# Dealing stretches of rows to SBUF partitions in another order in a row-wise maximum kernel

## The chip, the cores and the metric

The kernel runs on one core of one Trainium2 chip. The metric is the device time of one execution in microseconds (us), the median of several runs. One further execution was taken by the hardware profiler; the profile page and all views of the trace are of that one.

## The reference

The input `x` has 8192 rows of 8192 float32, 268.4 MB in all. The result is one number for each row, the largest absolute value in it:

```python
def reference(x: np.ndarray) -> np.ndarray:
    return np.linalg.norm(x, ord=np.inf, axis=1)
```

## The kernel before

**Layout.** Every row is reduced inside one SBUF partition. The rows are cut into two groups, `GROUPS = [46, 18]`. The first group is the first 46 x 128 rows of `x`, the second the remaining 18 x 128. Inside a group each partition has one stretch of neighbouring rows: 46 rows (1.5 MB, contiguous in `x`) in the first group, 18 rows (0.59 MB) in the second. Partition p has stretch p. This is made in lines 48 and 49: `x_of[f]` is a view of `x` with one row for each partition, its stretch, and `out_of[f]` is the same view of the result.

**Loads.** `load(pos, w)` (line 97) brings in the next `w` columns of every partition's stretch. It picks a place in `ring`, a tile with room for three loads of 16384 columns (64 KiB in each partition), and issues one transfer on SP's queue at line 108. The last load goes to a tile of its own, `last`. There are 39 loads. `WHOLE` lists the large ones: two of 8192 columns, thirty of 16384 (two rows of each partition, 8.39 MB), one of 8192. `LAST` lists the short ones that make up each partition's last row: 3920, 1984, 1040, 576, 320 and 352 columns. Since the loads use the ring in turn, a load may only be issued when the reduce of the load three places before it has ended; this wait stands on SP's queue ahead of the transfer. The calls to `declare_no_dep` at line 115 drop waits on earlier loads that those reduces already order.

**Reduces.** VectorE (DVE) does nearly all of the work: `absmax`, recorded at line 68, one instruction for each whole load, 128 partitions by one or two rows, into `res`, which has one column for each row of a partition. Near the end `shared` splits a row: VectorE takes its first part, while ScalarE (ACT, line 90) takes absolute values of the other parts and GpSimd (POOL, line 75) takes their maximum. Everything is emitted in a fixed order (`keep`).

**Stores.** When the last row is reduced (line 153), SP stores its 128 results at line 154. The other columns of `res` are stored a little earlier by two transfers from ScalarE's queue at line 159, one for each group. A store writes one run of numbers for each partition: 46 numbers in the first group, 17 in the second, and one in the last store.

Of the kernel before, what the change touches and what calls it, by code (L numbers as in the profile page):

```python
# [1 line left out]

# [4 lines left out]

P = 128
FP32 = mybir.dt.float32
INT32 = mybir.dt.int32  # L10
MAX = mybir.AluOpType.max
X = mybir.AxisListType.X
ABS = mybir.ActivationFunctionType.Abs

GROUPS = [46, 18]


WHOLE = (
    [(8192, ())] * 2 + [(16384, ())] * 29 + [(16384, (3712, 3680)), (8192, (2016, 1984))]
)
LAST = [
    (3920, (1680,)), (1984, (848,)), (1040, (432,)), (576, (240,)), (320, ()), (352, ())
]
RING = 3 * 16384


@with_exitstack  # L30
def kernel(
    ctx: ExitStack,
    tc: tile.TileContext,
    x: bass.AP,
    out: bass.AP,
):
    nc = tc.nc
    n_rows, n_cols = x.shape
    R = n_rows // P
    assert R == sum(GROUPS) and n_cols == 8192  # L40
    keep = tc.keep_in_program_order


    first = []
    x_of, out_of = {}, {}
    for k in GROUPS:
        f = len(first)
        x_of[f] = x[f * P : (f + k) * P].rearrange("(p r) m -> p (r m)", r=k)
        out_of[f] = out[f * P : (f + k) * P].rearrange("(p r) -> p r", r=k)
        first += [f] * k  # L50

    single = ctx.enter_context(tc.tile_pool(name="single", bufs=1))

    ring = single.tile([P, RING], FP32)
    res = single.tile([P, R], FP32)

    n_parts = sum(1 + len(g) for w, g in LAST[:-1])
    last = single.tile([P, LAST[-1][0] + n_parts], FP32)

    def not_before(inst, other, why):  # L60
        tc.add_manual_dep(
            inst.ins, other.ins.name,
            mybir.DependencyInfo(mybir.DependencyClass.Sync, mybir.DependencyReason.DATA),
            reason=why,
        )

    def absmax(dst, src):
        return keep(nc.vector.tensor_reduce(  # L68
            out=dst, in_=src, axis=X, op=MAX, apply_absolute_value=True,
        ))  # L70

    def max_pool(dst, src):

        pool = nc.gpsimd
        keep(pool.add_instruction(  # L75
            mybir.InstTensorReduce(
                name=nc.get_next_instruction_name(),
                ins=[pool.lower_ap(src.bitcast(INT32))],
                outs=[pool.lower_ap(dst.bitcast(INT32))],
                op=MAX,  # L80
                axis=X,
            )
        ))

    def shared(part, buf, g):

        a = buf.shape[1] - sum(g)
        red = absmax(part[:, :1], buf[:, :a])
        for i, c in enumerate(g):
            keep(nc.scalar.activation(buf[:, a : a + c], buf[:, a : a + c], ABS))  # L90
            max_pool(part[:, 1 + i : 2 + i], buf[:, a : a + c])
            a += c
        return red

    loads = []

    def load(pos, w):

        row = pos // n_cols
        a = pos - first[row] * n_cols  # L100
        if pos + w == R * n_cols:
            buf = last[:, :w]
        else:
            at = loads[-1][0] + loads[-1][1] if loads else 0
            if at + w > RING:
                at = 0
            buf = ring[:, at : at + w]
        inst = nc.sync.dma_start(out=buf, in_=x_of[first[row]][:, a : a + w]).ins  # L108
        if pos + w < R * n_cols:
            if (len(loads) + 4) % 10 < 5:  # L110


                for b, v, earlier in loads:
                    if b < at + w and at < b + v:
                        tc.declare_no_dep(
                            inst, earlier, reason="ordered by the reduces in between",
                        )
            loads.append((at, w, inst))
        return buf


    pos = 0
    for u, (w, g) in enumerate(WHOLE):
        buf = load(pos, w)
        row, k = pos // n_cols, w // n_cols
        pos += w
        whole = k - 1 if g else k
        if whole:
            red = absmax(
                res[:, row : row + whole],  # L130
                buf[:, : whole * n_cols].rearrange("p (c m) -> p c m", m=n_cols),
            )
        if g:
            part = single.tile([P, 1 + len(g)], FP32, name=f"part{u}")
            shared(part, buf[:, whole * n_cols :], g)
            max_pool(res[:, row + whole : row + k], part)
        if u == 1:

            not_before(
                keep(nc.scalar.activation(res[:, :1], res[:, :1], ABS)),  # L140
                red, "not before the second row is in",
            )


    n = LAST[-1][0]
    for h, (w, g) in enumerate(LAST[:-1]):
        buf = load(pos, w)
        pos += w
        shared(last[:, n : n + 1 + len(g)], buf, g)
        n += 1 + len(g)  # L150

    load(pos, LAST[-1][0])
    absmax(res[:, R - 1 :], last)
    final = nc.sync.dma_start(out=out_of[first[-1]][:, GROUPS[-1] - 1 :], in_=res[:, R - 1 :])


    for f, o in out_of.items():
        k = min(o.shape[1], R - 1 - f)
        early = keep(nc.scalar.dma_start(out=o[:, :k], in_=res[:, f : f + k]))
        tc.add_manual_dep(  # L160
            early.ins, final.ins.name,
            mybir.DependencyInfo(
                mybir.DependencyClass.NoSync, mybir.DependencyReason.SCHED_ONLY
            ),
            reason="takes the later semaphore",
        )


# [1 line left out]
_INS = ['x']  # L170
_OUTS = [((8192,), 'float32')]


# [23 lines left out]
```

## Time and profile before

| | |
|---|---|
| median of 3 runs | 627.39 us (627.34 to 627.58) |
| the profiled execution, whole | 627.43 us |
| its span, first to last instruction | 625.7 us |
| VectorE busy in the span | 536.7 us, 86% |
| ScalarE, GpSimd busy | 15.1 us, 14.1 us |
| bytes read from HBM | 268.44 MB |
| instructions | 175 |

The span is the part of an execution that the trace covers; the remaining 1.7 us lie around it. "Busy" is time in which an engine executes; a transfer's time "to landing" runs from its issue to the last of its bytes, and includes the time that it stands behind earlier transfers.

### The profile page before, as it was taken

The numbers are of one execution on the slowest core, as the hardware profiler recorded it, in microseconds if no ns is written. First come the engines' busy times: TensorE is split into PE (matmuls) and PEld (weight loads), VectorE is DVE, ScalarE is ACT, GpSimd is POOL, SyncE is SP. The second block draws the span as 40 slices with busy tenths as digits, with TensorE's granted clock in tenths as the row PEclk, the third lists the DMA queues.
The fourth block names the chain that finished last, engine by engine and source line by source line (L and its number), as shares of the span: only waits on it lengthen the run. The fifth ranks groups of instructions, "written<-read, shape, count | busy, mean of one in ns | idle before, by whom it ended". The sixth has DMA issues, their size and how long they took to land.

```text
span 625.7 us, 175 instructions
## 1 busy us (share of the span) xinstructions
DVE 536.7 (86%) x40; ACT 15.1 (2%) x10; POOL 14.1 (2%) x14
## 2 busy tenths in 40 slices
DVE  1938988889888899888898888988889888899888
ACT  0000000000000000000000000000000000000044
POOL 0000000000000000000000000000000000000026
DMA  8999999999999999999999999999999999999997
GB/s 369 436 469 402 469 402 469 402 469 402 469 402 457 415 415 457 402 469 402 469 402 469 402 469 402 469 402 453 419 415 457 402 469 402 469 402 469 402 436 304
DMA packets 6048, 268.47 MB, mean 429 GB/s; under 512 B 1056, under 2 KB 1312, under 8 KB 1696
## 3 DMA queue, kind: packets, MB, share of 16 engines
q1 hardware_dynamic: 5760, 268.44, 99.3%
q10 hardware_dynamic: 288, 0.03, 0.0%
HBM read 268.44 MB, written 0.03 MB: 429 GB/s over the span
## 4 chain that ended last, share of the span: by engine, by line
DMA 71%; DVE 28%; SPq 0%; issue 0%; DVEq 0%
DMA ring<-in_x_dram 71%; DVE res L68 28%; DVE last L68 1%; SPq L108 0%; DVEq L68 0%
## 5 line engine op out<-in xcount | busy, mean ns | idle before, releaser
L68 DVE TENSOR_REDUCE res<-ring 128x2 f32<-128x16384 f32 (+1 forms) x32 | 525.4, 16420 | 86.4 <-DMA ring<-in_x_dram 86.4
L90 ACT ACTIVATE ring<-ring 128x3712 f32<-128x3712 f32 (+7 forms) x8 | 13.6, 1719 | 577.2 <-DMA ring<-in_x_dram 573.9
L75 POOL TENSOR_REDUCE part<-ring 128x1 int32<-128x3712 int32 (+3 forms) x4 | 10.1, 2562 | 607.6 <-ACT ring L90 607.6
L68 DVE TENSOR_REDUCE part<-ring 128x1 f32<-128x800 f32 (+1 forms) x2 | 5.5, 2748 | 0.1
L68 DVE TENSOR_REDUCE last<-ring 128x1 f32<-128x2240 f32 (+4 forms) x5 | 5.3, 1115 | 0.1
L75 POOL TENSOR_REDUCE last<-ring 128x1 int32<-128x1680 int32 (+3 forms) x4 | 3.4, 855 | 0.6 <-ACT ring L90 0.4
L140 ACT ACT_TABLE_LOAD x1 | 1.3, 1283 | 0.7 <-PEq L181 0.7
L140 ACT ACTIVATE res<-res 128x1 f32<-128x1 f32 x1 | 0.2, 203 | 29.3 <-DVE res L68 29.3
L68 DVE TENSOR_REDUCE res<-last 128x1 f32<-128x361 f32 x1 | 0.5, 529 | 0.1
L75 POOL TENSOR_REDUCE res<-part 128x1 int32<-128x3 int32 x2 | 0.4, 198 | 0.1
L181 POOL MEMSET const-float32-0.0<- 128x1 f32 x1 | 0.1, 99 | 0.2 <-issue 0.2
L181 POOL MEMSET const-bfloat16-1.0<- 128x1 bf16 x1 | 0.1, 102 | 0.0
L181 POOL MEMSET const-uint8-127<- 128x1 uint8 x1 | 0.1, 101 | 0.0
L181 POOL MEMSET const-float32-1.0<- 128x1 f32 x1 | 0.1, 99 | 0.0
## 6 DMA issues: line engine op xcount, KB each, us to landing
ring<-in_x_dram SPq DMA_DIRECT2D x3, 4096.0 KB, 21.4
ring<-in_x_dram SPq DMA_DIRECT2D x1, 1960.0 KB, 35.4
ring<-in_x_dram SPq DMA_DIRECT2D x1, 992.0 KB, 37.4
ring<-in_x_dram SPq DMA_DIRECT2D x1, 520.0 KB, 38.2
ring<-in_x_dram SPq DMA_DIRECT2D x30, 40.8
ring<-in_x_dram SPq DMA_DIRECT2D x1, 288.0 KB, 38.4
last<-in_x_dram SPq DMA_DIRECT2D x1, 176.0 KB, 38.3
ring<-in_x_dram SPq DMA_DIRECT2D x1, 160.0 KB, 38.3
```

Of the source, the lines that this page charges most:

```text
L68: return keep(nc.vector.tensor_reduce(out=dst, in_=src, axis=X, op=MAX, apply_absolute_value=True,))
L75: keep(pool.add_instruction(mybir.InstTensorReduce(name=nc.get_next_instruction_name(), ins=[pool.lower_ap(src.bitcast(INT32))], outs=[poo ...
L90: keep(nc.scalar.activation(buf[:, a : a + c], buf[:, a : a + c], ABS))
L140: keep(nc.scalar.activation(res[:, :1], res[:, :1], ABS)),
L181: nc = _bacc.Bacc("TRN2", target_bir_lowering=False, num_devices=1)
```

## The change

In both groups the stretches are numbered q x 16 + g, with q from 0 to 7 and g from 0 to 15, and the view puts g ahead of q. The partition with number 8g + q thus has stretch 16q + g, instead of stretch 8g + q. The views have one axis more: `x_of[f]` has the axes (g, q, columns), `out_of[f]` has (g, q, rows). Each load reads the same bytes as before in the same number of pieces, and each row's result is stored in its place; the tiles, the reduces and the order of all instructions stay as they are.

```diff
     for k in GROUPS:
         f = len(first)
-        x_of[f] = x[f * P : (f + k) * P].rearrange("(p r) m -> p (r m)", r=k)
-        out_of[f] = out[f * P : (f + k) * P].rearrange("(p r) -> p r", r=k)
+        x_of[f] = x[f * P : (f + k) * P].rearrange("(q g r) m -> g q (r m)", g=16, r=k)
+        out_of[f] = out[f * P : (f + k) * P].rearrange("(q g r) -> g q r", g=16, r=k)
         first += [f] * k
...
-        inst = nc.sync.dma_start(out=buf, in_=x_of[first[row]][:, a : a + w]).ins
+        inst = nc.sync.dma_start(out=buf, in_=x_of[first[row]][:, :, a : a + w]).ins
...
-    final = nc.sync.dma_start(out=out_of[first[-1]][:, GROUPS[-1] - 1 :], in_=res[:, R - 1 :])
+    final = nc.sync.dma_start(out=out_of[first[-1]][:, :, GROUPS[-1] - 1 :], in_=res[:, R - 1 :])
...
     for f, o in out_of.items():
-        k = min(o.shape[1], R - 1 - f)
-        early = keep(nc.scalar.dma_start(out=o[:, :k], in_=res[:, f : f + k]))
+        k = min(o.shape[2], R - 1 - f)
+        early = keep(nc.scalar.dma_start(out=o[:, :, :k], in_=res[:, f : f + k]))
```

In the built program a load's destination was an access of 128 partitions by w elements and is now 128 by 1 by w; its source was 128 stretches by w and is now 16 by 8 stretches by w. A store's destination becomes 16 by 8 by its row count.

## The prediction, made before the changed kernel had run

> **What bounds the kernel now.** I read the page's busy table first (VectorE 86%, so no compute engine is full), then its DMA queues, then the chain of waits, then the waits of SP's queue, and last the stretch from 100 to 560 us alone.
>
> ```profile
> DVE 536.7 (86%) x40; ACT 15.1 (2%) x10; POOL 14.1 (2%) x14
> ...
> q1 hardware_dynamic: 5760, 268.44, 99.3%
> q10 hardware_dynamic: 288, 0.03, 0.0%
> ```
>
> The queue of loads has 99.3% of the time of all 16 DMA engines: 0.993 x 625.7 = 621.3 us, and 4.4 us of the span lie outside it. One engine moves 64 KiB in 621.3 / (268.44 MB / 16 / 65536 B) = 621.3 / 256 = 2.43 us, or 27.0 GB/s.
>
> ```profile
> DMA ring<-in_x_dram 71%; DVE res L68 28%; DVE last L68 1%; SPq L108 0%; DVEq L68 0%
> ...
> 59.17 40.78 DMA ring<-in_x_dram
> 99.95 0.02 issue
> 99.97 17.23 DVE res L68
> 117.20 0.02 issue
> 117.22 40.79 DMA ring<-in_x_dram
> 158.01 0.02 issue
> 158.03 17.23 DVE res L68
> ```
>
> The chain gives VectorE 28%, which misleads. A transfer takes 40.8 us from issue to landing, but 58.03 us go by for three loads, so loads land every 19.34 us and each waits about 21 us behind an earlier one. VectorE's 17.2 us lie on the chain only because they free the ring's place.
>
> ```profile
> SPq L108 <- DVE res L68: 517.7, 29, 19.0
> ...
> DVE res L68 <- DMA ring<-in_x_dram: 51.1, 24, 2.1
> ...
> 100.00:562.30 462.30, 413.24 (x24) 0.00 (x0) 0.00 (x0) 1.00 1.00 433
> ```
>
> (The first two lines are total us, times and longest of a wait, on SP's queue and in the steady part; the third is a stretch, its length, the busy time of DVE, ACT and POOL, the clock, the DMA share and GB/s.) In the steady part VectorE waits 2.1 us for each load and never the other way round; the engines' share is 1.00 at 433 GB/s. Thus the rate of the 16 DMA engines sets the time, and whatever lengthens a transfer shows at full size, since only 2.1 us of each period are VectorE's to give.
>
> [...]
>
> **The change, part by part.**
>
> Nothing is removed or moved: the same 39 loads and 3 stores, in the same places of the same queues, with the same bytes, no new wait. VectorE, ScalarE and GpSimd run as before.
>
> Issue of a transfer. SP's first load occupies its queue for 0.38 us, later ones 0.33 to 0.53. A two-axis source may take longer to set up; no row shows it. From below nothing, from above a doubling, 0.4. Loads in mid-stream have a load and more queued ahead (40.8 us to landing against 19.34 a load), so only the first load and the final store lie on the path: 0 to 0.8 us, and I take 0.4. The two stores on ScalarE's queue lie beside the last reduces; doubling them from 0.86 us together exposes at most the same again.
>
> Read order. Neighbours in g read places 46 x 32 KiB = 1.44 MiB apart (0.56 MiB in the second group). [...] to the start I allow 0.8 us more, since the first load lands 12.1 us after issue against 4.19 MB / 433 GB/s = 9.7 of payload. From the other side, clashes could cost[...]. I take 0.
>
> Write order, the part that decides. [...] The trace's packet records have the first packets of the 16 engines starting over 0.58 us[...]. I take 2.5%, near the small end[...].
>
> Sum on the profiled execution: stream 2 x 621.3 = 1242.6; less 2.5% of 621.3 = 15.5; plus the 4.4 us outside the stream and 0.4 for issue: span 1231.9. With 627.43 - 625.7 = 1.7 around it, 1233.6; I say 1233. The profiled execution is 0.04 us above the median shown, so nothing is corrected. VectorE's 17.2 us then fit into a period of about 38 us; what is late is always the load, also at the end, where the short loads land at half pace and VectorE no longer trails them.
>
> Range of this case: f from 6% (1212) to nothing (1249);[...] 1195 to 1255.
>
> **The rivals.**
>
> Partly staggered. [...] There are 64 segments of full size in the stream (268.44 MB / 16 / 4 / 64 KiB). [...] 660 to 1195.
>
> No effect. [...] Then only issue is left: 627.4 + 0.4 = 627.8. [...]
>
> A small loss on the read or write side, 1 to 5%[...]; range 629 to 660.
>
> Faster, the other side: [...] It decides when more than 1.25 us are won (0.2%). Against it: the stream's engines show a share of 1.00 at an even rate, with no sign that they wait for reads.
>
> **How the numbers follow.** Half rate 0.55, partly staggered 0.17, small loss 0.08, no effect 0.17, faster 0.03. The predicted time is that of the likeliest, 1233. The range from 634 to 1255 takes in the first two and most of the third, about 0.79. A change under 0.2% (1.25 us) is about what a measurement of this kernel cannot tell from none: slower by more 0.80, within 0.17, faster 0.03.
>
> **What would show it.** Right: loads' share near 100% with about half the GB/s, 217 to 222; loads landing every 38 us and about 80 us from issue; VectorE still 17.2 us a load and 537 in all, idle some 21 us before each; SP's queue waiting mostly for reduces, as now. Partly staggered: GB/s climbing along the 40 slices. No effect: 19.34 us a load throughout. SP's issues at more than 0.4 us show that part. It would be wrong at its root if loads land every 19.3 us[...]; wrong in size if the rate is even but well above 222 GB/s.

## The result, and the profile after

The changed kernel takes 1299.9 us (median of 6 runs, 1296.85 to 1303.27), against 627.43 us for the kernel before in the same comparison: 2.072 times as long, 95% interval 2.068 to 2.075. The profiled execution has a span of 1301.5 us.

From the changed kernel's page: the busy time of the engines, the rate in 40 slices, the queue of the loads, and the median time of a large load from issue to landing.

```profile
DVE 536.9 (41%) x40; ACT 15.1 (1%) x10; POOL 14.2 (1%) x14
...
GB/s 203 216 193 226 193 226 193 203 216 193 226 193 224 195 193 226 193 226 193 222 197 193 226 193 226 193 205 214 193 226 193 224 195 193 226 193 226 193 208 179
...
q1 hardware_dynamic: 5760, 268.44, 99.7%
...
ring<-in_x_dram SPq DMA_DIRECT2D x30, 104.4
```

The same 5760 packets move the same bytes, and the 16 engines are again busy all the time, 99.7%. They just move half as much in that time, evenly from the first slice to the last. The stretch from 100 to 600 us (bounds, length, busy time of VectorE, ScalarE and GpSimd with their instructions, clock, DMA share, GB/s):

```profile
100.00:600.00 500.00, 208.16 (x13) 0.00 (x0) 0.00 (x0) 1.00 1.00 207
```

A load takes 104.4 us to land, since it stands behind two others that are as slow.

The chain of waits in the changed kernel (start, length, what):

```profile
84.31 17.22 DVE res L68
101.53 23.30 another core or an unknown queue
124.83 0.02 issue
124.85 17.22 DVE res L68
142.07 23.31 another core or an unknown queue
```

A reduce starts every 40.54 us, where it was 19.34. VectorE's own 17.22 us have not changed. The 23.3 us between two reduces go to "an unknown queue" only because this view does not name transfers as long as these; those of 40.8 us in the kernel before it does name. The list of waits (total us, times, longest) says what ended them, first in the kernel before, then in the changed one:

```profile
DVE res L68 <- DMA ring<-in_x_dram: 86.4, 32, 12.8
```

```profile
DVE res L68 <- DMA ring<-in_x_dram: 743.3, 32, 31.8
```

VectorE waits 743 us for loads where it waited 86. With the 10.5 and 8.1 us for which its last short reduces now wait for loads too, that is the 676 us by which the span has grown. So all of the loss is in the rate of the loads. It is no stall at one place: in the trace's packet records a piece of 64 KiB (one packet, two rows in one partition) takes 2.42 us in the kernel before, each of them, and 5.07 us on average in the changed one (4.94 for the first of every four, 5.12 for the other three).

One smaller thing shows in the list of what line 108 issues (ns, shortest, median, longest). First the kernel before, then the changed one:

```profile
L108 SPq DMA_DIRECT2D ring<-in_x_dram x38: 327/328/532, 0.7 to 583.9; - x38
```

```profile
L108 SPq DMA_DIRECT2D ring<-in_x_dram x38: 536/537/646, 0.7 to 1199.3; - x38
```

A transfer with a two-axis source takes SP 0.54 us to issue in place of 0.33.

### The profile page after: what moved, and what is told of

Read it like the earlier page. It is cut to its first block, busy times and chain, and to the rows that moved or that the text cites. A ratio compares the mean times of both kernels' runs of the same rounds, so it can differ in the third digit from the quotient of the medians.

```text
span 1301.5 us, 175 instructions
## 1 busy us (share of the span) xinstructions
DVE 536.9 (41%) x40; ACT 15.1 (1%) x10; POOL 14.2 (1%) x14
## 3 DMA queue, kind: packets, MB, share of 16 engines
q1 hardware_dynamic: 5760, 268.44, 99.7%
## 4 chain that ended last, share of the span: by engine, by line
another core or an unknown queue 56%; DVE 41%; DMA 3%; issue 0%; SPq 0%; DVEq 0%
DVE res L68 40%; DMA ring<-in_x_dram 3%; DVE last L68 0%; DVE part L68 0%; SPq L108 0%; DVEq L68 0%
## 5 line engine op out<-in xcount | busy, mean ns | idle before, releaser
L90 ACT ACTIVATE ring<-ring 128x3712 f32<-128x3712 f32 (+7 forms) x8 | 13.6, 1719 | 1231.4 <-DMA ring<-in_x_dram 1217.8
L68 DVE TENSOR_REDUCE part<-ring 128x1 f32<-128x800 f32 (+1 forms) x2 | 5.5, 2750 | 10.5 <-DMA ring<-in_x_dram 10.5
## 6 DMA issues: line engine op xcount, KB each, us to landing
ring<-in_x_dram SPq DMA_DIRECT2D x30, 104.4
```

The source lines that it names most:

```text
L68: return keep(nc.vector.tensor_reduce(out=dst, in_=src, axis=X, op=MAX, apply_absolute_value=True,))
```

## The experiments

Theory 1 is that of the prediction, and its estimate: in the changed kernel engines hold each other up, two and two, as they write to SBUF, whatever the order of the stretches. No view shows which engine writes which partition, and the runs test the theory by the rate alone. Its factor 2 and its f are estimates too. f is the lead of one engine over another, as a share of a segment, by which the author means four pieces of 64 KiB (4 x 2.42 = 9.7 us in the kernel before); a segment was to take (2 - f) x 9.7 us, with f at most 6%, from the 0.58 us over which the first packets start. Theory 2 blames the reads: neighbouring stretches clash in HBM. Theory 3 is a mixture, since the slowdown is more than 2. Kernels that were run once have one time and no interval; the differences read from them are large.

### The old order, with a source of two axes

```diff
-        x_of[f] = x[f * P : (f + k) * P].rearrange("(p r) m -> p (r m)", r=k)
+        at = min(f * P, n_rows - 16 * (8 * k + 1))
+        x_of[f] = (
+            x[at : at + 16 * (8 * k + 1)]
+            .rearrange("(g s) m -> g s m", g=16)[:, : 8 * k]
+            .rearrange("g (q r) m -> g q (r m)", r=k)
+        )
```

> The source has two axes, 16 x 8, as in the changed kernel, but the stretches go to the partitions in the old order (partition p has stretch p). To keep the two axes apart in the built program, each block of 8 stretches starts one row further on, so the results are those of rows shifted by up to 15 rows. Theory 1[...]: the order of the stretches does not matter, so about 1300 us, a load every 40.5 us. Theory 2, reads of neighbouring stretches clash in HBM: the old distances between the engines' reads are back, so about 628 us, a load every 19.3 us. Theory 3, both take part[...]: a load every 38.7 us, about 1245 us.

Measured: 1302.16 us. From its chain of waits:

```profile
327.55 17.22 DVE res L73
344.77 23.28 another core or an unknown queue
368.05 0.02 issue
368.07 17.22 DVE res L73
```

Again a load every 40.52 us, with the stretches where they were in the kernel before. The order in which `x` is read, which is all that the change is about in words, has no visible part in the loss (1302.16 us in the old order, 1299.9 in the changed one); it comes with the access of 16 by 8 stretches. Theory 2 and the mixture fall.

### Groups of four partitions

```diff
-        x_of[f] = x[f * P : (f + k) * P].rearrange("(q g r) m -> g q (r m)", g=16, r=k)
-        out_of[f] = out[f * P : (f + k) * P].rearrange("(q g r) -> g q r", g=16, r=k)
+        x_of[f] = x[f * P : (f + k) * P].rearrange("(q g r) m -> g q (r m)", g=32, r=k)
+        out_of[f] = out[f * P : (f + k) * P].rearrange("(q g r) -> g q r", g=32, r=k)
```

> The change with g from 0 to 31 and q from 0 to 3: partition 4g + q has stretch 32q + g. The source still has two axes and stretches read side by side are still neighbours in x, but a share is now four partitions[...]. Theory 1[...] full rate comes back, a load every 19.3 us, 627.4 to 628.5 us, with SP's issues at 0.54 us as in the changed kernel; if the groups are dealt in pairs of neighbours, still about 1300. Theory 2 (neighbouring reads clash in HBM): slow as the changed kernel, 1200 us or more. Theory 3: the reads' part stays, some 4.8% over before, 655 us.

Measured: 628.49 us (21 runs), 1.0017 times the kernel before, interval 1.0010 to 1.0023. Its stretch from 100 to 600 us, and the start of its chain of waits:

```profile
100.00:600.00 500.00, 446.00 (x26) 0.00 (x0) 0.00 (x0) 1.00 1.00 432
```

```profile
0.73 0.64 SPq L108
...
2.05 40.60 DMA ring<-in_x_dram
42.65 0.02 issue
42.67 17.23 DVE res L68
```

The full rate is back, with a two-axis source and with neighbouring stretches read side by side; a piece of 64 KiB takes 2.42 us as in the kernel before. So neither of these two is dear. What decides is the cut: 432 GB/s with 32 groups of four, 207 with 16 groups of eight. Why it does was not shown, for no view tells which engine wrote what. What remains, 1.1 us, arises at the two ends, where nothing hides it: the first load takes 0.64 us to issue against 0.38 and its bytes have landed 0.77 us later than before; the last store takes 0.61 against 0.35 and lands after 1.8 us against 1.4. This version too deals the stretches in another order, and it is still 0.17% slower than the kernel before.

### Two halves, old order and one axis

```diff
-        inst = nc.sync.dma_start(out=buf, in_=x_of[first[row]][:, a : a + w]).ins
+        halves = [
+            nc.sync.dma_start(out=buf[h : h + 64], in_=x_of[first[row]][h : h + 64, a : a + w]).ins
+            for h in (0, 64)
+        ]
```

The declarations at line 115 are left out in this kernel, so its loads keep the waits on earlier loads.

> The kernel before with each load cut into two transfers, partitions 0 to 63 and 64 to 127, each with the old one-axis source and old order. [...] Theory 1[...]: about half rate without any change of order; a pair of halves takes 38.7 us[...] (about 1245 us in all), 40.5 us[...] (about 1300). Theory 2 (reads): about 630 us, since the reads are as before.

Measured: 1300.71 us, a pair of halves every 40.48 us. The same stretch of its trace:

```profile
100.00:600.00 500.00, 208.09 (x13) 0.00 (x0) 0.00 (x0) 1.00 1.00 208
```

This kernel makes the same slowdown from another side. The order and the axes are those of before; a transfer writes 64 partitions in place of 128, and the rate is 208 GB/s in place of 433. It also gives the size: 40.5 us a load here too, not 38.7. So the loss beyond the factor 2 doesn't need the changed order.

### Delaying some engines

These runs test the rest of the theory: if engines hold each other up because they start together, a lag of one segment (256 KiB) between them should bring the rate back while the loads themselves stay as they are. Two short copies within HBM are to make the lag, one of 12 rows and one of 4. The trace bears out the counts (in the first run below 12 engines end the first copy at 8.5 to 9.1 us, and 4 end the second at 13.6 to 14.0). Which engines they are (the lowest-numbered or others), and which two hold each other up (partners below), no view shows; the copies were laid out by the author's estimate of both.

```diff
+    lag = 4 * LAG
+    scratch = nc.dram_tensor("scratch", (16, lag), FP32).ap()
+    for lo, n in ((0, 12), (12, 4)):
+        nc.sync.dma_start(
+            out=scratch[lo : lo + n].rearrange("p (c m) -> p c m", c=4),
+            in_=x[lo * 8 : (lo + n) * 8].rearrange("(p r) m -> p (r m)", r=8)[:, :lag].rearrange("p (c m) -> p c m", c=4),
+        )
     loads = []
```

> The changed kernel with two short HBM-to-HBM copies ahead of the first load[...], 128 KiB for each engine. [...] by the time of one such copy, 4.8 us at 27 GB/s or about 9.7 us at half of that[...]. Theory 1 with its lead that is kept: f is 0.5 to 1 in place of 0.02, so a load every 29 us (f = 0.5) down to 19.4 us (f = 1), 640 to 980 us in all, for a copy of some 10 us. Theory 2 (reads)[...]: about 1310 us, the changed kernel's time and the copies'.

Measured, with `LAG = 8192` (128 KiB for each engine): 1286.58 us, a load every 40.07 us.

```profile
100.00:600.00 500.00, 214.66 (x13) 0.00 (x0) 0.00 (x0) 1.00 1.00 209
```

A miss. The records of completions show that the lag was made and kept: in every load from the first to the last, 4 engines end first, 8 about 5.4 us later, 4 about 11 us. But it was a lag made at half rate: of the 20 us that a segment takes here, 5.4 are f = 0.27, not 0.5. Even at f = 0.27 the estimate's (2 - f) asks for about 34 us a load, and nearly nothing came. If a conflict anywhere slows all engines, that is to be expected, for a lag of 5.4 us leaves 14.6 of the 20 us of a segment in which partners overlap.

Two runs with longer copies followed, the first with copies of 12 and of 4 rows, the second with one of 8. Theory 1a adds that one pair in conflict holds up all engines; by theory 1b the lags do not part the pairs, or the cause is another:

> As the run staggered, with copies of 256 KiB for each engine, so that by the landing times of that run (5.2 us between groups for 128 KiB) the groups lie about 10 us apart, close to the 9.7 us of four partitions at full rate (f near 1). In the run staggered the lead was kept through all loads and still nothing was gained. Theory 1a[...]: at f = 0.5 one half of the pairs is in conflict at any time, so all are held; at f near 1 no pair is ever in conflict, so a load every 19.4 to 22 us and 650 to 750 us in all. Theory 1b[...]: still a load about every 40 us, about 1290 us.

> The control of staggered_full: one copy of 256 KiB for each of the lowest-numbered 8 engines[...]. Theory 1a: partners still meet, no gain, a load every 40 to 40.5 us, about 1300 us. [...]

Both were void: 1308.98 and 1304.38 us, but the landings of each load lay within 1.2 us, so no engine lagged. With 256 KiB for each row the copies' source was one contiguous run, and all 16 engines shared it (16 end each copy). They were made again with gaps between the rows (`x[lo * 16 : (lo + n) * 16]` and `r=16` in the lines above, `LAG = 16384`), and a third was made with one copy of 4 rows:

> staggered_full again: there the copies' source was one contiguous run and went to all 16 engines, so no group lagged (landings of one load within 1.2 us). Here the copies read rows with gaps between, so that they stay on 12 and 4 engines: 256 KiB for each, groups some 10 us apart, f near 1. Theory 1a[...]: no pair in conflict, a load every 19.4 to 22 us, 650 to 750 us in all. Theory 1b[...]: a load every 40 us, about 1290 us.

> The control again with a copy that stays on 8 engines[...]. Theory 1a: about 1300 us, a load every 40 to 40.5 us. [...]

> One copy of 256 KiB for each of the lowest-numbered 4 engines[...]. In the first two large loads, before any load has to wait for a reduce: [...] all need some 5 us. The end time is set by the slower pairs in either case, about 1290 to 1310 us.

| run | engines delayed | gaps between landings, us | us a load | time, us |
|---|---|---|---|---|
| staggered_full_2 | 12, then 4 | 4 first, 8 about 9.6 later, 4 about 19.6; from 185 us on 3 first, 1 about 6.7 later, 7 about 9.7, 5 about 19.5 | 29.0 | 953.02 |
| lowest_8_delayed_2 | 8 | 8 first, 8 about 9 later | 40.4 | 1309.93 |
| lowest_4_delayed | 4 | 12 first, 4 about 9.4 later | 40.2 | 1296.67 |

The same stretch in each, in the order of the table:

```profile
100.00:600.00 500.00, 296.36 (x18) 0.00 (x0) 0.00 (x0) 1.00 1.00 288
```

```profile
100.00:600.00 500.00, 218.57 (x13) 0.00 (x0) 0.00 (x0) 1.00 1.00 207
```

```profile
100.00:600.00 500.00, 217.41 (x13) 0.00 (x0) 0.00 (x0) 1.00 1.00 208
```

Delaying 8 engines gains nothing (40.4 us a load). Its lag is only about half a segment (9 of 20 us), but had every engine's partner been in the other eight, all would have been clear of each other at once for nearly half of the time. By theory 1 some partners are therefore in the same eight. Delaying 12 and then 4 gains 347 us (953.02 against 1299.9), though less than expected. In its first 190 us one of the first four engines fell back by some 6 us, and one of the eight fell back to the last group; whether this cost the rest was not tried. Delaying 4 shows one thing more: 4 engines are then half a segment behind the other 12 (9.4 of 20 us), yet the share of all 16 is 1.00, and all pieces of the large loads that follow take 4.8 to 5.1 us. Had pairs been on their own, those that the lag parts would have needed 2.4 us in part and stood idle in the end. Neither the 4 nor the 12 were spared. In staggered_full_2 it shows in time: the 16 engines' pieces that start at 302 us take 2.4 to 2.6 us, those that start at 304 and 305 us 4.1 to 4.8.

The last of this kind puts the copies where segments have their full size:

```diff
+        if len(loads) == 2:
+            delay(0, 12)
+            delay(12, 4)
         inst = nc.sync.dma_start(out=buf, in_=x_of[first[row]][:, :, a : a + w]).ins
```

Here `delay` makes one of the two copies above, of 4 x 13568 numbers a row for the 12 and 4 x 15872 for the 4. The copies of all these runs read 4.2 MB or less beside the 268.4 of the loads, and nothing reads what they write.

> The changed kernel with the two copies put after the second load, [...] so that each takes about 9.7 us by the packets of staggered_full_2 and falls where the segments have their full size. [...] So each group should lie one whole segment behind the next (in staggered_full_2 a load took 29.1 us, which with a common slowdown of 2.095 whenever any pair is in conflict means f = 0.77). Theory 1a: f near 1, no conflict, a load every 19.4 to 22 us and 660 to 740 us in all. If a stagger can only help in part for another reason, a load every 29 us again, about 950 us.

Measured: 806.73 us. The rate in 40 slices:

```profile
GB/s 205 208 379 313 352 326 332 365 326 329 358 319 358 355 322 361 342 335 365 345 335 365 365 365 365 378 401 368 384 381 378 371 410 368 378 388 375 252 200 100
```

The first two slices, before the copies, run at the changed kernel's 205 GB/s. From the third to the 37th it is 313 to 410: a load every 24.7 us at first and 22.0 at the end, with more than half of the pieces of 64 KiB at 2.42 to 2.6 us. Two copies of about 10 us save 493 of the 672 us that the changed kernel loses, with the loads themselves as they were. Most of the loss thus depends on when the engines run. The expected 660 to 740 us were not reached; the groups' landings lie about 9.7 us apart at first and 9.4 at the end, short of one segment, which takes 12.4 us and then 11.0. These are averages: the eight engines in the middle end over 1.9 us at first and over 3.3 us later.

### What the loss beyond the factor 2 belongs to

Against the kernel with two halves, and like it without the declarations at line 115:

```diff
-            nc.sync.dma_start(out=buf[h : h + 64], in_=x_of[first[row]][h : h + 64, a : a + w]).ins
-            for h in (0, 64)
+            nc.sync.dma_start(out=buf[h : h + 16], in_=x_of[first[row]][h : h + 16, a : a + w]).ins
+            for h in range(0, 128, 16)
```

> The kernel before with each load cut into eight transfers of 16 partitions[...]. [...] twice the time and 5.6% more in the changed kernel (5.11 us for 64 KiB against 2 x 2.42) and the same in two_halves. [...] 64 KiB take 4 x 2.42 x 1.056 = 10.2 us, a load every 82 us, about 2620 us in all; if it grows with each further writer, more, at 15% 2850 us; [...] 9.7 us and 2490 us.

Measured: 2389.34 us.

```profile
100.00:600.00 500.00, 104.61 (x7) 0.00 (x0) 0.00 (x0) 1.00 1.01 113
```

Below all three values: a transfer of 16 pieces of 64 KiB, to 16 partitions, takes 9.32 us with all engines busy (share 1.01), 3.85 times the 2.42 of the kernel before. This is less than the whole number 4 that the expectation started from, where the 5.12 us of the changed kernel are 2.11 times, more than 2. So the 5.6% are not added to every slowdown of this kind.

The other run takes every second partition of 16 (`buf[h + b : h + 16 : 2]` with b = 0, 1), so that a transfer has eight pieces:

> The kernel before with each load cut into 16 transfers of 8 partitions, every second one of 16[...]. It asks where the 5.6% beyond the factor 2 come from, which four_writers did not show (64 KiB in 9.33 us there, 3.86 times 2.42). [...] 5.11 us for 64 KiB, 16 x 5.11 = 81.8 us a load, about 2620 us. [...] 4.67 to 4.84 us, 75 to 77.5 us a load, 2390 to 2480 us.

Measured: 1663.21 us. From its page:

```profile
GB/s 112 125 112 118 120 120 123 123 136 129 136 140 128 148 136 144 151 156 166 144 145 169 191 215 215 218 210 221 216 215 215 215 216 207 222 216 218 155 97 24
...
q1 hardware_dynamic: 10128, 268.46, 48.7%
```

A miss of another kind. Eight engines are busy (48.7% of 16). They begin at 112 GB/s and climb by themselves to 216, the full rate of eight engines (8 x 27.1): it looks as if engines drift apart here, which is an estimate from the rate. From 100 to 300 us a fifth of the pieces take 5.05 to 5.12 us, as in the changed kernel; at 156 and at 165 us, for instance, four pieces that start within 0.7 us of each other take 5.11. So a piece can take that long with only eight engines busy. Why four_writers comes out below its multiple of 2.42 us is open.

## Why the prediction was right in its case and wrong in its size

Right, by its own steps: the loads' rate bounds the kernel, with nothing else near it (DMA share 1.00 at 207 GB/s, VectorE unchanged at 536.9 us). The order of the reads, for which it took 0, does not decide: 1302.16 us with the old order in old_order_two_axes, 628.49 with neighbouring stretches side by side in groups_of_4. Half rate was its likeliest case and slower its forecast, at 0.80. That the loss arises where the engines write was the author's estimate. It agrees with the runs: 64 partitions at a time are written at 208 GB/s with the reads of before (two_halves), and a lag between engines brings 313 to 410 back (staggered_late). But what holds the engines up was not shown.

The step that failed is the factor of exactly 2, which stands in the sum as the stream term: 2 x 621.3 less 15.5 for the lead, 1227.1 us. Measured, the loads' queue has 99.7% of the profiled 1301.5 us, 1297.6: 70.5 us more. This is the whole miss of the profiled execution, for what lies outside the stream came out as 3.9 us against 4.8. The term took for granted that engines which hold each other up move together half of what they moved before, and no less. An engine got 12.8 GB/s (64 KiB in 5.117 us, the later three of four pieces), where half of the old 27.1 is 13.5. A segment of four pieces would take 4 x 5.117 = 20.47 us without a lead, where twice the old rate is 8 x 2.421 = 19.37; over 64 segments the difference is 70 us. The range of 1255 had no room for it, since no bound was put on how far below half the rate can fall.

Nothing in the trace of before told this factor. The run two_halves, with the order and the axes of before, measures it: 40.48 us a load against 19.35, 2.09.

Two smaller readings were off without bearing on the sum. The three loads of the lines shown take 58.06 us (99.97 to 158.03), not 58.03. And a load is issued when the reduce three places back has ended, so it lands three periods less one reduce later: by the prediction's own period 3 x 38.3 - 17.2 = 98 us, not the 80 given as a sign; measured, 3 x 40.54 - 17.2 = 104.4.

The lead was near in size for the changed kernel (the first of four pieces is 0.17 us shorter, 64 x 0.17 = 11 us against 15.5), but its rule, each pair on its own with (2 - f), is not right: at f = 0.27 almost nothing was gained (40.07 us a load against 40.54), and in lowest_4_delayed, where 4 engines lag by 9.4 us, no engine was faster than the others (4.8 to 5.1 us a piece).

The rival "partly staggered" didn't come about: the rate is even over the span (193 to 226 GB/s in all but the last slice). Something like it shows in two_writers_four_ports, where the rate climbs by itself from 112 to 216. "No effect" fell with 207 GB/s in place of 433. "Faster" and "small loss" counted on HBM: groups_of_4 reads neighbouring stretches side by side, as the change does, at 432 GB/s, so there was nothing to win or lose. The cost of issue, taken as 0.4 us with bounds of 0 and 0.8, measures 1.08 us in groups_of_4 (628.49 against 627.41; by the interval of the ratio 0.6 to 1.4 us, so the bound of 0.8 is not clearly passed). The issue itself is 0.26 us longer at each end; the rest came after it, in the time to the first bytes and to the store's landing, which the prediction left out.

## What to carry to other kernels

In this kernel the way in which the axes of a transfer are cut changed its rate by a factor 2.07, with the same bytes in the same number of pieces. A reading that fits the runs, though no view shows it, is that the cut decides which partitions are written at the same time, and with that how far the engines hold each other up. A view that permutes rows should therefore be tried with more than one cut: here 128 partitions in one axis or 32 groups of four ran at full rate (433 and 432 GB/s), and 16 groups of eight at half (207). When all engines are busy and the rate is half, as here, look at the duration of a packet (5.07 us against 2.42) and not at waits.

## What the runs showed of the hardware that was not expected

- With transfers to 64 partitions a load took 40.48 us (two_halves), with transfers to 16 partitions 8 x 9.32 = 74.6 (four_writers), against 19.35 with 128: 2.09 and 3.85 times as long. The first is above the factor 2, the second below the factor 4 that had been expected at the least.
- With 4 of 16 engines delayed by 9.4 us all pieces took 4.8 to 5.1 us (lowest_4_delayed), those of the 4 as those of the 12. The runs show only the slowdown, not its path.
- A lag between engines, once made, stayed through 30 loads and 1200 us to within half a microsecond in 14 of the 16 engines (run staggered), while in staggered_full_2 two engines fell back by some 6 us before all was steady, and in two_writers_four_ports the rate climbed from 112 to 216 GB/s. What decides between these was not tried.
- A two-axis source costs 0.2 us more of SP's time for each transfer (0.54 against 0.33), which matters only at the two ends.
